# The output gate stored as rows, and the latents split a granule later, in a decoder layer on one core

## The chip, the core and the metric

The kernel runs on one core of one Trainium2 chip. The core has a matrix engine (TensorE, PE in the profile), a vector engine (VectorE, DVE), an activation engine (ScalarE, ACT), GpSimd (POOL), and a sync engine (SyncE, SP) that issues most transfers here. Each engine works through its own queue of instructions in order, and semaphores tie the queues together. Transfers run on 16 DMA engines. TensorE accumulates into PSUM, eight banks of 128 x 512 float32; everything else works in SBUF, 128 partitions wide.

The metric is the device time of one execution in microseconds (us), the median of several.

## The reference

One layer of a decoder with two token mixers in parallel, for one sequence of 512 tokens, D = 2048, in float32.

```python
shift, scale, gate = split(silu(c) @ w_ada + b_ada, 3)        # c: one vector of 2048 for the sequence
h = rmsnorm(x, attn_norm_g) * (1 + scale) + shift
q_lat, kv_lat, k_rope, z_mla, u, v, z_sgu, g_mla, g_sgu = split(h @ w_in)   # widths 768, 512, 64, 6 x 2048

# A: causal attention, 16 heads, from normalised latents
q  = rmsnorm(q_lat, q_norm_g) @ w_uq          # per head 128 + 64 rotary
kv = rmsnorm(kv_lat, kv_norm_g) @ w_ukv       # per head 128 (k) + 128 (v)
y_mla = attention(q, [k | rope(k_rope)], v) * silu(z_mla)
# B: spatial gating in chunks of 128 tokens, 16 groups
y_sgu = u * (tril(w_spatial) @ rmsnorm(v, sgu_norm_g) + b_spatial) * silu(z_sgu)

merged = sigmoid(g_mla) * y_mla + sigmoid(g_sgu) * y_sgu
out = rmsnorm(x + gate * (merged @ w_out), final_norm_g)
```

## The kernel before

**Precision.** Every float32 product is made of three TensorE matmuls on high and low halves (`mm3`: high x high, high x low, low x high). ScalarE makes the high half by a cast, VectorE the low half by a subtraction (`hilo`). Weights come through `Stream`: SP loads 512 KB pieces into three raw buffers in turn (`wraw`, line 98), ScalarE casts each (L117), VectorE subtracts (L118), into one of two pairs, `w0h`/`w0l` and `w1h`/`w1l`. `get(i, ahead)` splits up to piece i + ahead and lets SP load as far as there are free raw buffers. `load_before(piece, f)` hangs another transfer into SP's queue just ahead of that piece's load. SP's queue is in order: an issue that waits for a semaphore holds everything behind it.

**Stages.** In the profiled execution the vectors and the first projection columns come first, then the column blocks (to about 1087 us), the attention heads (to about 1410), the output projection (to the end).

**Column blocks.** The other columns of `h @ w_in` are made in 11 blocks of 28 granules, each granule 24 matmuls, in a scheme that saves products by sums of quarters of the weights. So ScalarE and VectorE split many sums there (ScalarE casts at L620, VectorE subtractions recorded at L135). Everything else that has to happen beside this is in a table of events: `on(s, phase, f)` sets a function at granule s, where s counts up to 0, the first step of attention. In each granule the phases run in the order

```python
FIRST, HIGH, EVAC, GATE, SPLIT, BACK, MISC, LOAD = range(8)
```

with the granule's matmuls between BACK and MISC. The order of the calls is the order in each engine's queue. Ten latent vectors (`latn_d`, 128 x 512 each, six for q and four for k and v) are normalised earlier and kept in DRAM. Near the end of the blocks they come back: `lat_fetch(i)` loads one into a tile `b`, and `lat_split(i)` makes its high half `hh` on ScalarE (scaled by a gain) and its low half `hl` on VectorE. `first_weights` loads the first attention weights, and `split_to(gr[0])` splits the first of them.

**Attention.** Sixteen heads, each with projections of q, k and v from the latents, scores, softmax, transposes, the product with v (`pv`) and the merge with the other mixer. The last head has no next head to prepare; in the places of its projections it runs the first three granules of the output projection.

**Output projection.** The product with `w_out` has four groups of 512 columns, cg = 0 to 3; the first three are done in eight granules each, i = 0 to 7 (`out_granule`, 24 matmuls in four PSUM banks, banks 0 to 3 and 4 to 7 in turn). Granules (0,0), (0,1) and (0,2) lie in the last head, so 21 follow it. Weights `go[cg, i]` come through `Stream` and some of the fourth group's among them. The list `later` holds functions that are called after a granule, by the step 8 * cg + i - 3. The fourth group is done row block by row block at the end, each followed by the final norm and the store of its output rows.

**The gate.** The third part of the adaLN vector is made late. Element j * 128 + p of it is the dot product of row j * 128 + p of the transposed `w_ada` with silu(c). VectorE makes these as multiply-and-sum over a 128-row chunk (one column of `dots` for each of 16 chunks), so the gate comes out as columns: chunk j is column j of `gate`, one element in each partition. The first 8 columns (NG = 8) are made in pieces of 512 during the heads (`piece_sum`); after the last head a reduction over the four pieces and `gate_sum`, which adds the bias, finish them. The other eight follow during the output projection (`chunk_load`, `chunk_sum`) at the steps of `chunk_at` (5, 7, 9, 10 for columns 8 to 11; 11 to 14 for columns 12 to 15).

The residual step needs the gate along the free axis, the same in all partitions. So it goes through DRAM: `gate_store` writes columns a to b to `gate_row`, and `grow_load(cg)` reads 512 of them back as one row broadcast to 128 partitions (`grow`, named `gbc` in the trace). SP issues both. For the first eight columns both stand right behind the last head; then come the gain vector, and, hung between the weight loads of the next granules, `cact` (silu(c), 1 MB), the four row blocks of `xn` (x again, 1 MB each) and the first chunks. For column groups 2 and 3 the store stands one step behind the last `chunk_sum` of the group and the load one step behind that.

Of the kernel before, what the change touches and what calls it, by code (L numbers as in the profile page):

```python
# [11 lines left out]
F32 = mybir.dt.float32  # L12
# [4 lines left out]
ALU = mybir.AluOpType  # L17
AX = mybir.AxisListType
PSUM = bass.MemoryType.PSUM

P = 128
D = 2048
S = 512
KC = D // P
# [18 lines left out]
V7 = [(p, i) for i in range(4) for p in (1, 6)] + [(p, i) for i in range(4) for p in (2, 7)]  # L43
# [8 lines left out]
NG = 8  # L52
# [75 lines left out]
def trunk_layer(ctx, tc, xT, xn, c, vecs, pos, wada, w1, w2, wv, wv3, wv4, wh, wh15, wq, wqr, wk, wvv, wo, wsT, bsp, gfin, out,  # L128
                dbg=None):
    nc = tc.nc  # L130
    ACT, DVE, PE, DMA = nc.scalar, nc.vector, nc.tensor, nc.sync
    LEFT, RIGHT = "left", "right"

    def tt(out, in0, in1, op):
        DVE.tensor_tensor(out=out, in0=in0, in1=in1, op=op)  # L135
# [32 lines left out]
    def nt(p, shape, dt, tag, **kw):  # L168
        uid[0] += 1
        return p.tile(shape, dt, tag=tag, name=f"{tag}_{uid[0]}", **kw)  # L170
# [11 lines left out]
    ws = Stream(nc, [(wp, f"wraw{i}") for i in range(3)], [(wp, f"w{i}") for i in range(2)])  # L182
# [8 lines left out]
    ident = nt(cst, [P, P], F32, "ident")  # L191
# [13 lines left out]
    gate = nt(cst, [P, KC], F32, "gate")  # L205
    dots = nt(cst, [P, 3 * KC], F32, "dots")
# [11 lines left out]
    def scratch(name, shape):  # L218
        return dram.tile(shape, F32, name=name, tag=name)

    gate_row = scratch("gate_row", [KC, P])
# [43 lines left out]
    gq, gr, gk, gvv = {}, {}, {}, {}  # L265
# [45 lines left out]
    def get(i, ahead=1, run=1):  # L311
        r = ws.get(i, ahead)
        fs, pend[:] = pend[:run], pend[run:]
        for f in fs:
            f()
        return r
# [8 lines left out]
    def bank_at(k):  # L325
        return nt(psp.p, [P, S], F32, f"ps{k}")

    def bank():
        n_bank[0] += 1
        return bank_at(ring[(n_bank[0] - 1) % len(ring)])  # L330
# [333 lines left out]
    def gate_sum(a, b):  # L664

        cols = slice(a, b)
        tt(gate[:, cols], dots[:, 2 * KC + a:2 * KC + b], vec[:, C_BADA + 2 * KC + a:C_BADA + 2 * KC + b], ALU.add)

    def gate_store(a, b):
        DMA.dma_start(gate_row[a:b].rearrange("k p -> p k"), gate[:, a:b])  # L670

    def v_norm():
        DVE.tensor_reduce(out=rv, in_=ssv, axis=AX.X, op=ALU.add)
# [15 lines left out]
    FIRST, HIGH, EVAC, GATE, SPLIT, BACK, MISC, LOAD = range(8)  # L689

    def on(s, phase, f, *a):
        assert s >= done[0], (s, done)
        events.setdefault(s, {}).setdefault(phase, []).append(lambda: f(*a))
# [7 lines left out]
    def place(s, us, f, *a):  # L701

        def full(s):
            own, (a, b) = busy.get(s, 0.0) + us, (busy.get(s + d, 0.0) for d in (-1, 1))
            return own > 3.3 or own + max(a, b) > 5.75

        while full(s):
            s += 1
        spend(s, us)
        on(s, BACK, f, *a)  # L710
        return s
# [11 lines left out]
    n_v = len(V7)  # L723
# [28 lines left out]
    rows = {}  # L752
# [199 lines left out]
    for g in range(H):  # L952
# [3 lines left out]
        a = s_ + 4  # L956
        on(a, BACK, sgu_scale)
        a = place(a, 0.29, sgu_weights)
        a = place(a, 0.29, sgu_weights_split)
        if g + 1 < H:  # L960
            on(a + 1, LOAD, sgu_load, g + 1)
        a = place(max(a, s_ + 5), 0.69, sgu_gain)
        a = place(a + 1, 0.69, sgu_split)
# [233 lines left out]
    for group in (((10, "lat8"), (11, "lat9")), ((12, "lat10"), ("plain", "sinT"))):  # L1197
# [9 lines left out]
        i = group[0][0]  # L1207
# [107 lines left out]
    s_att = max(V7.index((2, 3)) + 1 - n_v, s_lat + 1)  # L1315
    on(s_att, LOAD, to_attention)
    for i in range(10):
        on(s_att + i // 2, LOAD, lat_fetch, i)
        on(V7.index((3, 3)) + 1 - n_v + i // 2 if i < 8 else -4, BACK, lat_split, i)

    def first_weights(n):
        ws.limit = gr[0] + n
# [1 line left out]

    for n, s_ in enumerate((-7, -5, -3, -1)):
        on(s_, LOAD, first_weights, n)
    on(-1, SPLIT, lambda: ws.split_to(gr[0]))
    on(-1, MISC, lambda: ws.split_to(gq[0]))
    ws.next_raw, ws.next_part = 0, 1

# [2 lines left out]
    for b in range(len(BLOCKS)):  # L1333
        if b == 1:
            ring[:], n_bank[0] = [5, 6], 0
        for g, (p, i) in enumerate(V7):
# [23 lines left out]
            for k in range(2):  # L1360
                xh, xl = rights[p](2 * i + k)
                st, sp = i == k == 0 and p in (1, 5, 6), i == 3 and k == 1
# [41 lines left out]
    partial = dots[:, 0:4 * NG].rearrange("p (j q) -> p j q", q=4)  # L1404
# [21 lines left out]
    def pieces_at(h):  # L1426
        k = (2 * h, 26, 26, 29)[max(h - 12, 0)]
        for i in range(k, k + (2, 0, 3, 3)[max(h - 12, 0)]):
            piece_sum(i)
# [202 lines left out]
    def out_granule(cg, i, banks, ahead=1, run=1):  # L1632
        wH, wL = get(go[cg, i], ahead, run)
        for k in range(2):
            j = 2 * i + k
            sl = slice(k * 512, (k + 1) * 512)
            for n in range(NB):
                tk = slice(n * P, (n + 1) * P)
                mm3(banks[n], mh[j][:, tk], ml[j][:, tk], wH[:, sl], wL[:, sl], j == 0, j == H - 1)

    for h in range(H):
        if h == H - 1:
            ring[:], n_bank[0] = [4, 5, 6, 7], 0
        dst = scores(h)
        more, odd = h + 1 < H, h % 2 == 1
        pair = h // 2 + 1
        first = go[0, 0] if not more else gr[pair] if not odd and 2 * pair < H else None
        pr_, shares_ = softmax(h, dst, (lambda: ws.split_to(first)) if first is not None else None)
        if more:
            qproj(h + 1, lambda: merge(1 if h == H - 2 else None))  # L1650
            if not odd and 2 * pair < H:
                rps = rproj(pair)
        else:
            pso = [bank_at(k) for k in range(NB)]
            for i in range(2):
                out_granule(0, i, pso)
        pa, fa = transposes(pr_, (0,))
        fa()
        if h < GATED:
            for n in range(NB):  # L1660
                g_ = gt[h][:, n * P:(n + 1) * P]
                ACT.activation(g_, g_, AF.Copy, scale=shares_[:, n:n + 1])
        pb, fb = transposes(pr_, (1,))
        fb()
        pc, fc = transposes(pr_, (2, 3))
        fc()
        if more:
            kps = kproj(h + 1)
            kfinish(h + 1, kps)
        else:  # L1670
            merge()
            pieces_at(h)
            out_granule(0, 2, pso)
        gate_ = gt[h]
        if h < GATED:
            gate_ = nt(tp, [P, S], F32, "sig", bufs=3)
            ACT.copy(gate_, turn(gt[h]))
        tps = turn(vt[h])
        ops = pv(h, {**pa, **pb, **pc})
        merge_a(h, ops, tps, gate_)  # L1680
        if not odd:
            pieces_at(h)
        if not odd and 2 * pair < H:
            m2 = at("m2", F32)
            swapped(m2, rps)
        if more and odd:
            rfinish(pair, rps, m2)
            vproj(pair)
    merge()
    DVE.tensor_reduce(out=dots[:, 2 * KC:2 * KC + NG], in_=partial, axis=AX.X, op=ALU.add)  # L1690
    gate_sum(0, NG)
    gate_store(0, NG)
    gd.close()
    hp.close()
    latp.close()
# [10 lines left out]
    chunks, later = {}, {}  # L1706
# [16 lines left out]
    chunk_at = dict(zip(range(NG, KC), (5, 7, 9, 10, 11, 12, 13, 14)))  # L1723
    for j, st in chunk_at.items():
        later.setdefault(st, []).append(lambda j=j: chunk_sum(j))
        if j + 2 < KC:
            later[st].append(lambda j=j: chunk_load(j + 2))
    for cg in range(NG // 4, 4):
        st = chunk_at[4 * cg + 3]
        later.setdefault(st + 1, []).append(lambda cg=cg: gate_store(4 * cg, 4 * cg + 4))  # L1730
        later.setdefault(st + 2, []).append(lambda cg=cg: grow_load(cg))
    for j in range(NG, NG + 2):
        load_before(go[1, j - NG], chunk_load, j)
# [147 lines left out]
```

## Time and profile before

| | us |
| --- | --- |
| median of 3 runs (1593.01, 1593.63, 1597.45) | 1593.63 |
| the profiled execution | 1595.34 |
| its span in the trace | 1593.60 |
| TensorE busy | 1563.6 (98% of the span) |
| VectorE busy | 1220.5 (77%) |
| ScalarE busy | 801.4 (50%) |
| GpSimd busy | 69.5 (4%) |

The mean clock that TensorE was granted was 0.994 of full speed. The DMA engines moved 316.16 MB, on average 198 GB/s over the span. The profiled execution's time is 1.74 us longer than its span, for what lies around the program. All times of views are in us from the start of the span; line numbers are those of the kernel before. A matmul at a lowered clock counts as busy for longer, so the busy share alone does not say how much of the time is lost.

### The profile page before, as it was taken

How to read it: one execution, taken by the hardware profiler on the slowest of the kernel's cores; microseconds unless marked ns; L12 is line 12 of the kernel's file. 1: busy time of each engine (PE TensorE's matmuls, PEld its weight loads, DVE VectorE, ACT ScalarE, POOL GpSimd, SP SyncE). 2: the span in 40 equal slices, each digit the busy share in tenths (PEclk: the TensorE clock that was granted, in tenths of full speed). 3: DMA queues.
4: the chain of work that ended last, by engine and by line, in shares of the span. 5: the costliest groups of instructions: out<-in, count | busy, mean ns of one | idle time of the engine just before them, and what ended most of it. 6: DMA issues, size and time to landing. Idle time of an engine off the chain costs nothing. (4 is left out here: it accounts for less than half of the span.)

```text
span 1593.6 us, 20601 instructions
## 1 busy us (share of the span) xinstructions
PE 1563.6 (98%) x7397; PEld 1299.8 (82%) x7397; DVE 1220.5 (77%) x1662; ACT 801.4 (50%) x1238; POOL 69.5 (4%) x67
## 2 busy tenths in 40 slices
PE   8999999999999999999999999999999999999998
PEld 7888778888888878888888888877888888878777
DVE  7989777677888889788888788777777778836643
ACT  4445555546544546454545564656566655422222
POOL 0000000201010101020201010100000000000000
PEclk9999999999999999999999999999999999999999
DMA  9979575949695969695948596865333434248722
GB/s 381 360 265 345 164 196 164 245 133 289 214 230 170 237 194 236 193 235 180 229 146 237 183 241 195 215 215 175 120 116 110 126 110 127 89 143 332 207 84 106
DMA packets 239288, 316.16 MB, mean 198 GB/s; under 512 B 18281, under 2 KB 186257, under 8 KB 233553
## 3 DMA queue, kind: packets, MB, share of 16 engines
q1 hardware_dynamic: 216130, 291.25, 55.9%
q0 software_dynamic: 22912, 23.07, 9.5%
q8 instruction: 58, 0.95, 0.3%
q10 hardware_dynamic: 144, 0.52, 0.1%
q14 instruction: 44, 0.36, 0.1%
HBM read 291.11 MB, written 23.68 MB: 198 GB/s over the span
## 5 line engine op out<-in xcount | busy, mean ns | idle before, releaser
L135 DVE TENSOR_TENSOR X<-X,X 128x1024 fp32r<-128x1024 f32 (+2 forms) x110 | 129.4, 1181 | 29.5 <-ACT X L620 26.6
L620 ACT CAST w0h<-X 128x1024 fp32r<-128x1024 f32 x70 | 73.6, 1051 | 95.0 <-PE ps L1366 61.4
L620 ACT CAST X<-X 128x1024 fp32r<-128x1024 f32 x69 | 72.5, 1051 | 89.7 <-PE ps L1366 54.0
L620 ACT CAST w1h<-X 128x1024 fp32r<-128x1024 f32 x70 | 73.6, 1052 | 82.5 <-PE ps L1366 44.2
L135 DVE TENSOR_TENSOR w0l<-X,w0h 128x1024 fp32r<-128x1024 f32 x70 | 85.5, 1221 | 27.1 <-ACT w0h L620 26.8
L135 DVE TENSOR_TENSOR w1l<-X,w1h 128x1024 fp32r<-128x1024 f32 x70 | 85.5, 1222 | 26.1 <-ACT w1h L620 25.6
L118 DVE TENSOR_TENSOR w0l<-wraw,w0h 128x1024 fp32r<-128x1024 f32 (+4 forms) x61 | 64.2, 1053 | 53.3 <-ACT w0h L117 51.6
L147 PE MATMUL ps<-hh,w1h 128*128 128x512 f32 (+1 forms) x260 | 103.4, 398 | 1.7 <-ACT hh L425 1.4
L148 PE MATMUL ps<-hl,w1h 128*128 128x512 f32 (+1 forms) x260 | 101.6, 391 | 0.5 <-DVE hl L138 0.5
L149 PE MATMUL ps<-hh,w1l 128*128 128x512 f32 (+1 forms) x260 | 101.5, 391 | 0.0
L117 ACT CAST w0h<-wraw 128x1024 fp32r<-128x1024 f32 (+4 forms) x61 | 55.9, 917 | 83.6 <-issue 21.9
L135 DVE TENSOR_TENSOR X<-wraw,X 128x1024 f32<-128x1024 f32 (+1 forms) x66 | 80.6, 1221 | 19.6 <-ACT X L620 17.0
L1367 PE MATMUL ps<-w1l,hh 128*128 128x512 f32 x236 | 92.3, 391 | 2.5 <-DVE w1l L135 2.5
L1367 PE MATMUL ps<-w0l,hh 128*128 128x512 f32 x236 | 92.3, 391 | 1.8 <-DVE w0l L135 1.7
L147 PE MATMUL ps<-hh,w0h 128*128 128x512 f32 x238 | 93.7, 394 | 0.0
L148 PE MATMUL ps<-hl,w0h 128*128 128x512 f32 x238 | 92.8, 390 | 0.0
L149 PE MATMUL ps<-hh,w0l 128*128 128x512 f32 x238 | 92.7, 390 | 0.0
L1365 PE MATMUL ps<-w0h,hh 128*128 128x512 f32 x236 | 92.1, 390 | 0.1
L1365 PE MATMUL ps<-w1h,hh 128*128 128x512 f32 x236 | 91.9, 390 | 0.2 <-ACT w0h L620 0.2
L138 DVE SCALAR_TENSOR_TENSOR wada<-wada,cact 128x2048 f32<-128x2048 f32 x39 | 88.9, 2282 | 4.1 <-DMA wada<-in_wada 4.1
L1366 PE MATMUL ps<-w0h,hl 128*128 128x512 f32 x236 | 91.9, 389 | 0.0
L1366 PE MATMUL ps<-w1h,hl 128*128 128x512 f32 x236 | 91.9, 389 | 0.0
(395 smaller groups left out, 4348.9 us busy)
## 6 DMA issues: line engine op xcount, KB each, us to landing
X<-in_wh SPq DMA_DIRECT2D x131, 512.0 KB, 4.7
wada<-in_wada SPq DMA_DIRECT2D x39, 1024.0 KB, 7.7
wraw<-in_wo SPq DMA_DIRECT2D x32, 512.0 KB, 5.0
wraw<-in_wh SPq DMA_DIRECT2D x21, 512.0 KB, 5.6
wraw<-in_wh POOLq DMA_DIRECT2D x21, 512.0 KB, 8.1
X<-in_wv SPq DMA_DIRECT2D x17, 512.0 KB, 3.7
X<-in_wh SPq DMA_DIRECT2D x22, 384.0 KB, 3.6
half<-in_w SPq DMA_DIRECT2D x32, 256.0 KB, 5.2
```

The lines of the kernel that those rows point to most:

```text
L117: self.nc.scalar.copy(hi[:, :n], raw[:, :n])
L118: self.nc.vector.tensor_tensor(out=lo[:, :n], in0=raw[:, :n], in1=hi[:, :n].bitcast(F32), op=ALU.subtract)
L135: DVE.tensor_tensor(out=out, in0=in0, in1=in1, op=op)
L138: DVE.scalar_tensor_tensor(out=out, in0=in0, scalar=scalar, in1=in1, op0=op0, op1=op1, **kw)
L147: PE.matmul(ps, ah, bh, start=start, stop=False)
L148: PE.matmul(ps, ah, bl, start=False, stop=False)
L149: PE.matmul(ps, al, bh, start=False, stop=stop)
L620: ACT.copy(hi, t)
L1365: PE.matmul(ps[t].rearrange("p (h w) -> p h w", h=4), xh[:, tk], wH[:, k], start=st, stop=False, skip_group_check=True)
L1366: PE.matmul(ps[t].rearrange("p (h w) -> p h w", h=4), xl[:, tk], wH[:, k], start=False, stop=False, skip_group_check=True)
L1367: PE.matmul(ps[t].rearrange("p (h w) -> p h w", h=4), xh[:, tk], wL[:, k], start=False, stop=sp, skip_group_check=True)
```

## The change

**The gate.** `gate_store` is gone. In its place `gate_turn` lets TensorE transpose the finished columns (128 x 8 or 128 x 4) into a PSUM bank, and VectorE copies the result (8 x 128 or 4 x 128) to a tile `sig`; SP then writes rows of 128 consecutive elements to `gate_row`. For the first eight columns the reduction and `gate_sum` stand ahead of granule (0,2) in the last head, and the turn and store right behind that granule. For groups 2 and 3 the turn stands where the store stood, in a bank named by number (1 and 4), the store a step later, and `grow_load` a step after that, one step later than before.

**The latents.** `lat_fetch` is called for three latents in a granule instead of two. `lat_split` of two latents a granule moves from granules -8 to -4 to granules -7 to -3. In granule -1, `split_to(gr[0])` goes from phase SPLIT to phase HIGH.

```diff
--- before.py
+++ after.py
@@ -666,8 +666,11 @@
         cols = slice(a, b)
         tt(gate[:, cols], dots[:, 2 * KC + a:2 * KC + b], vec[:, C_BADA + 2 * KC + a:C_BADA + 2 * KC + b], ALU.add)
 
-    def gate_store(a, b):
-        DMA.dma_start(gate_row[a:b].rearrange("k p -> p k"), gate[:, a:b])
+    def gate_turn(a, b, pg, row):
+
+        PE.transpose(pg[:b - a, :P], gate[:, a:b], ident)
+        DVE.tensor_copy(row[:b - a, :P], pg[:b - a, :P])
+        return lambda: DMA.dma_start(gate_row[a:b], row[:b - a, :P])
 
     def v_norm():
         DVE.tensor_reduce(out=rv, in_=ssv, axis=AX.X, op=ALU.add)
@@ -1315,8 +1318,8 @@
     s_att = max(V7.index((2, 3)) + 1 - n_v, s_lat + 1)
     on(s_att, LOAD, to_attention)
     for i in range(10):
-        on(s_att + i // 2, LOAD, lat_fetch, i)
-        on(V7.index((3, 3)) + 1 - n_v + i // 2 if i < 8 else -4, BACK, lat_split, i)
+        on(s_att + i // 3, LOAD, lat_fetch, i)
+        on(i // 2 - 7, BACK, lat_split, i)
 
     def first_weights(n):
         ws.limit = gr[0] + n
@@ -1324,7 +1327,7 @@
 
     for n, s_ in enumerate((-7, -5, -3, -1)):
         on(s_, LOAD, first_weights, n)
-    on(-1, SPLIT, lambda: ws.split_to(gr[0]))
+    on(-1, HIGH, lambda: ws.split_to(gr[0]))
     on(-1, MISC, lambda: ws.split_to(gq[0]))
     ws.next_raw, ws.next_part = 0, 1
 
@@ -1670,7 +1673,10 @@
         else:
             merge()
             pieces_at(h)
+            DVE.tensor_reduce(out=dots[:, 2 * KC:2 * KC + NG], in_=partial, axis=AX.X, op=ALU.add)
+            gate_sum(0, NG)
             out_granule(0, 2, pso)
+            gate_turn(0, NG, bank(), nt(tp, [P, S], F32, "sig", bufs=3))()
         gate_ = gt[h]
         if h < GATED:
             gate_ = nt(tp, [P, S], F32, "sig", bufs=3)
@@ -1687,9 +1693,6 @@
             rfinish(pair, rps, m2)
             vproj(pair)
     merge()
-    DVE.tensor_reduce(out=dots[:, 2 * KC:2 * KC + NG], in_=partial, axis=AX.X, op=ALU.add)
-    gate_sum(0, NG)
-    gate_store(0, NG)
     gd.close()
     hp.close()
     latp.close()
@@ -1725,9 +1728,12 @@
         later.setdefault(st, []).append(lambda j=j: chunk_sum(j))
         if j + 2 < KC:
             later[st].append(lambda j=j: chunk_load(j + 2))
-    for cg in range(NG // 4, 4):
-        st = chunk_at[4 * cg + 3]
-        later.setdefault(st + 1, []).append(lambda cg=cg: gate_store(4 * cg, 4 * cg + 4))
+    rows = []
+    for cg, k in ((2, 1), (3, 4)):
+        st = chunk_at[4 * cg + 3] + 1
+        later.setdefault(st, []).append(lambda cg=cg, k=k: rows.append(
+            gate_turn(4 * cg, 4 * cg + 4, bank_at(k), nt(tp, [P, S], F32, "sig", bufs=3))))
+        later.setdefault(st + 1, []).append(lambda: rows.pop()())
         later.setdefault(st + 2, []).append(lambda cg=cg: grow_load(cg))
     for j in range(NG, NG + 2):
         load_before(go[1, j - NG], chunk_load, j)
```

The next rows show the queues of three engines as written, before and now. A row names the line, the operation, the tiles written and read, and the size.

VectorE in the last head, before. `piece` and `dots` are the gate's last partial sums, `w0l` and `w1l` low halves of split weights, the first `sig` the merge of the head, `dots` at L1690 the reduction and `gate` the finished columns:

```order
L138 SCALAR_TENSOR_TENSOR piece_12118,dots_93<-piece_12118,cq_11389 128x512
L118 TENSOR_TENSOR w0l_12266<-wraw_99_12076,w0h_12265 128x1024
L135 TENSOR_TENSOR sig_12313<-ps_1851_12300,g_1787_11810 128x512
L135 TENSOR_TENSOR sig_12313<-sig_12313,ps_1850_12295 128x512
L135 TENSOR_TENSOR g_1854_12317<-sig_12313,b_1853_12316 128x512
L1690 TENSOR_REDUCE dots_93<-dots_93 128x8
L135 TENSOR_TENSOR gate_92<-dots_93,vec_88 128x8
```

And the same place now (the `sig` of 8x128 is the gate as rows, the others the merge):

```order
L138 SCALAR_TENSOR_TENSOR piece_12118,dots_93<-piece_12118,cq_11389 128x512
L1676 TENSOR_REDUCE dots_93<-dots_93 128x8
L135 TENSOR_TENSOR gate_92<-dots_93,vec_88 128x8
L118 TENSOR_TENSOR w0l_12268<-wraw_99_12076,w0h_12267 128x1024
L672 COPY sig_12298<-ps_1850_12297 8x128
L135 TENSOR_TENSOR sig_12320<-ps_1853_12307,g_1787_11810 128x512
```

The reduction and the sum moved from behind the merge to ahead of the split of a weight, and the copy of the turned gate is new between that split and the merge.

SP at the store of column group 2, before (`wraw`: weight loads, `wada`: a chunk for later gate columns, `gbc`: the row read back):

```order
L670 DMA gate_row<-gate_92 128x4x1
L98 DMA wraw_115_12765<-in_wo 128x1024
L1714 DMA wada_12792<-in_wada 128x2048
L1710 DMA gbc_12329<-gate_row 128x512
L98 DMA wraw_116_12807<-in_wo 128x1024
```

And SP at the same place now:

```order
L673 DMA gate_row<-sig_12765 4x128
L98 DMA wraw_116_12814<-in_wo 128x1024
L98 DMA wraw_117_12816<-in_wo 128x1024
L1713 DMA gbc_12333<-gate_row 128x512
L98 DMA wraw_118_12852<-in_wo 128x1024
```

The store now stands behind the weight load and the chunk load that it was ahead of, and two further weight loads stand between it and the load that reads it.

ScalarE at the first latents, near the end of the column blocks, before (`X` and `w1h`: high halves of column weights, `hh`: high halves of latents, `d`: an activation of a result):

```order
L620 CAST X_1328_8668<-X_1310_8578 128x1024
L1295 ACTIVATE hh_1330_8675<-b_1317_8618,vec_88 128x512
L1295 ACTIVATE hh_1332_8679<-b_1318_8620,vec_88 128x512
L620 CAST w1h_8701<-wraw_1236_8104 128x1024
L844 ACTIVATE d_1285_8401<-d_1285_8401 128x1024
```

And ScalarE at the same place now:

```order
L620 CAST X_1331_8674<-X_1310_8578 128x1024
L620 CAST w1h_8697<-wraw_1236_8104 128x1024
L847 ACTIVATE d_1285_8401<-d_1285_8401 128x1024
L1298 ACTIVATE hh_1338_8702<-b_1317_8618,vec_88 128x512
L1298 ACTIVATE hh_1340_8706<-b_1318_8620,vec_88 128x512
```

The first pair of latent halves moved behind one cast of a column weight and one activation.

## The prediction

> **What bounds the kernel now.** I read the page's engine line first, then busy time by stretches, then TensorE's waits, then the chain of waits behind them.
>
> ```profile
> PE 1563.6 (98%) x7397; PEld 1299.8 (82%) x7397; DVE 1220.5 (77%) x1662; ACT 801.4 (50%) x1238; POOL 69.5 (4%) x67
> ```
>
> TensorE is the bound, and every matmul is needed. This change adds three small ones and removes none, so it can only win what TensorE loses: idle time and a lowered clock. The next table shows where. Its columns are start:end and length, busy time and count of PE, PEld, DVE, ACT and POOL, granted clock, DMA share, GB/s.
>
> ```profile
> 1100.00:1380.00 280.00, 279.21 (x1669) 247.56 (x1668) 216.40 (x460) 161.68 (x373) 0.00 (x0) 1.00 0.39 123
> 1458.40:1485.60 27.20, 27.20 (x121) 22.52 (x120) 20.83 (x22) 7.44 (x10) 0.00 (x0) 1.00 0.82 274
> 1418.86:1535.26 116.40, 105.85 (x433) 84.90 (x432) 62.75 (x66) 30.02 (x40) 0.00 (x0) 0.94 0.76 248
> 1061.18:1087.00 25.82, 22.98 (x97) 17.71 (x96) 22.77 (x28) 18.32 (x25) 0.00 (x0) 1.00 0.56 189
> ```
>
> The attention heads lose nothing. The second row is the output projection undisturbed: five granules of 24 matmuls in 27.20 us, 5.44 us each or 0.2267 us a matmul. The third row is 18 granules of it, 432 matmuls (the 433rd hangs over the edge): 18 x 5.44 = 97.92, so 116.40 - 97.92 = **18.5 us are lost**. The fourth row is the end of the column blocks, just ahead of attention: 96 x 0.2267 = 21.76, so **4.1 us are lost**. TensorE's waits, first in 1380 to 1594, then in 1000 to 1110:
>
> ```profile
> PE ps L147 <- ACT w0h L117: 5.6, 2, 3.2
> PE ps L147 <- ACT w1h L117: 2.5, 1, 2.5
> PE ps L1367 <- DVE w0l L135: 1.4, 1, 1.4
> PE ps L1367 <- DVE w1l L135: 1.3, 1, 1.3
> ```
>
> In the projection it waits for weights to be split, and the splits wait for loads. The chain there, in order of time (start, length), and SP's own wait:
>
> ```profile
> 1411.28 10.51 DMA gate_row<-gate
> 1427.68 16.74 DMA wraw<-in_wo
> ...
> 1479.85 11.54 DMA gate_row<-gate
> 1491.88 6.09 DMA wraw<-in_wo
> ...
> 1509.37 10.11 DMA wraw<-in_wo
> SPq L1710 <- DMA gate_row<-gate: 21.6, 3, 10.1
> ```
>
> Each column store of the gate takes 10.5 to 11.5 us to land, SP waits 21.6 us for them at `grow_load`, and all weight loads stand behind it in SP's queue. The store also holds up what is issued after it: the load of 1509.37 took 10.1 us with SP free. In the three stretches behind the stores the DMA engines moved almost nothing:
>
> ```profile
> 1412.50:1421.50 9.00, 9.00 (x41) 7.45 (x40) 2.45 (x2) 2.11 (x2) 0.00 (x0) 1.00 0.05 2
> 1485.50:1491.50 6.00, 6.00 (x29) 4.95 (x27) 3.76 (x3) 1.05 (x1) 0.00 (x0) 1.00 0.96 75
> 1510.00:1517.50 7.50, 7.50 (x35) 6.21 (x34) 3.69 (x5) 1.78 (x3) 0.00 (x0) 1.00 0.51 32
> ```
>
> The first only waits; in the other two loads were queued (share 0.96 and 0.51) and moved 75 and 32 GB/s.
>
> **Part 1: the gate as rows.** The three stalls, two granules each (10.88 us if undisturbed), a fourth small one, and the clock behind the three:
>
> ```profile
> 1424.30:1441.35 17.05, 13.09 (x49) 10.07 (x48) 2.45 (x2) 2.09 (x2) 0.00 (x0) 0.90 1.01 399
> 1491.04:1507.19 16.15, 12.87 (x49) 9.98 (x48) 9.16 (x12) 4.95 (x7) 0.00 (x0) 0.89 0.74 237
> 1512.63:1529.82 17.19, 14.29 (x49) 10.90 (x48) 9.15 (x11) 5.42 (x8) 0.00 (x0) 0.80 0.63 177
> 1452.24:1458.40 6.16, 5.76 (x25) 4.43 (x24) 5.06 (x7) 1.66 (x3) 0.00 (x0) 1.00 0.83 301
> 1435.30:1438.65 3.35, 3.35 (x10) 2.57 (x9) 0.00 (x0) 0.38 (x1) 0.00 (x0) 0.50 1.03 429
> 1500.15:1503.50 3.35, 3.07 (x7) 2.48 (x8) 3.32 (x5) 1.23 (x2) 0.00 (x0) 0.50 0.52 157
> 1520.65:1527.40 6.75, 6.25 (x14) 4.59 (x15) 5.67 (x7) 2.61 (x4) 0.00 (x0) 0.50 0.51 168
> ```
>
> They cost 6.2, 5.3, 6.3 and 0.7 us, together the 18.5. Of these, 13.45 us at half clock are 6.7 us. [...] The waits here were 3.2, 2.5 and 2.4 us and the clock fell after all three, so I follow the trace: no gap, no half clock.
>
> The new store has a twin in this kernel, the turn of the SGU gains to rows:
>
> ```profile
> 265.38:271.32 5.94, 5.94 (x27) 4.65 (x26) 3.57 (x4) 2.42 (x4) 0.00 (x0) 1.00 0.43 132
> L766 SPq DMA_DIRECT2D gain_row<-sig x1: 329/329/329, 268.9 to 268.9; - x1
> DMA to landing us min/median/max: 1.4/1.4/1.4
> L765 ACT COPY vec<-ps x1: 158/158/158, 268.7 to 268.7; 128x16 f32<-128x16 f32 x1
> ```
>
> A 16-row store landed in 1.4 us. Two transposes lengthened 24 matmuls (5.44) to 5.94, 0.25 us each; three cost **0.7 us** (0.3 if they hide in the group of four that follows the first, 1.5 if each waits for VectorE). The copies out of PSUM are bounded by that 0.16 us copy and by a 128x512 multiply, 0.69 us. VectorE at the last head, before (start, length, idle ahead):
>
> ```profile
> 1404.85 1.22 DVE L118 TENSOR_TENSOR w0l<-wraw,w0h 128x1024 fp32r<-128x1024 f32 x1
> 1408.11 0.69 DVE L135 TENSOR_TENSOR sig<-ps,g 128x512 f32<-128x512 f32 x1 [2.04 <-PE ps L149]
> 1410.87 0.18 DVE L1690 TENSOR_REDUCE dots<-dots 128x8 f32<-128x32 f32 x1
> 1411.08 0.17 DVE L135 TENSOR_TENSOR gate<-dots,vec 128x8 f32<-128x8 f32 x1
> ```
>
> Its 2.0 us idle ahead of the merge hold the copy (first pair of order rows, with the change). Sum and gate moved up from behind the merge, ahead of `w0l`, and the copy stands where the idle time was. The copy waits for TensorE to end granule 2; the merge behind it waits longer anyway, for the `pv` matmuls. `w0l` is 0.35 us later and TensorE needs it after `pv`, so that is covered too. On SP (second pair of order rows, at the second store) the store moved behind a weight load and a chunk load, and two more weight loads, each held by a split, stand between it and its reader, a granule apart: 5.4 us against 1.4. The third store gains the same distance. Its copy stands ahead of two splits on VectorE and waits for the end of granule (2,2); those splits are due a granule later, so the delay is covered. If one of the two came late, its granule would stall as the second does now. The first store now leaves near 1407 (1404.85 + 0.35 + 1.22, the copy and the issue) and lands near 1409 instead of 1421.8, so `grow_load`, the vectors, `xn` and the weights go out some 12 us earlier. I take all **18.5 us** (bounds: 12.3 if the first stall stays, 18.5).
>
> **Part 2: the latents split a granule later.** What stalled there, ScalarE in order of time:
>
> ```profile
> 1065.95 1.38 ACT L1295 ACTIVATE hh<-b,vec 128x512 fp32r<-128x512 f32 x2 [2.01 <-DMA b<-latn_d]
> 1067.23 1.04 ACT L620 CAST w1h<-wraw 128x1024 fp32r<-128x1024 f32 x1
> 1069.98 1.39 ACT L1295 ACTIVATE hh<-b,vec 128x512 fp32r<-128x512 f32 x2 [0.75 <-DMA b<-latn_d]
> 1071.27 1.03 ACT L620 CAST w0h<-X 128x1024 fp32r<-128x1024 f32 x1
> 1078.28 1.04 ACT L620 CAST w1h<-X 128x1024 fp32r<-128x1024 f32 x1
> ```
>
> The first `hh` sits in the queue 2.0 us before its latent lands, and the casts of the column weights wait behind it. In the third pair of order rows (`X`, `w1h`: column weights; `hh`: latent halves; `d`: an activation of a result) a latent pair no longer stands ahead of a `w1h` cast. The first pair moved behind a cast and an activation, and every later pair likewise, with its VectorE half. SP's third fetch passes one column-weight load, which goes out an issue (0.4 us) later and is cast only at 1078. Following both queues with these lengths (1.0 a cast, 0.66 a split half), `w0h` ends near 1068.6 instead of 1072.3 and its stall goes (4.1 split as the waits, 1.4 to 1.3, is 2.1 and 2.0). `w1h` ends near 1076.8 instead of 1079.3, but TensorE arrives 2.1 us sooner, so I leave about 1 us there and 0.3 at the last granule: 4.1 - 1.3 = **2.8 us** gained (bounds: 4.1 if all is covered, 1.5 lost if the last pair, now at -3, delays the first attention weights). Moving the first attention split ahead on VectorE covers that.
>
> **Sum.** 18.5 - 0.7 + 2.8 = 20.6 us. The profiled execution took 1595.34 (span 1593.60 and 1.74 around it); 1595.3 - 20.6 = **1574.7 us**. The median of the runs, 1593.63, is 1.7 below that execution, about what half of one 3.35 us half-clock stretch costs. I sum against the profiled execution, since the lost time is measured in it.
>
> **Rivals.**
> - *The first stall returns as a burst* (0.10). The rows (0.75 MB), `cact` (1 MB), two chunks and `xn` (1 MB each piece) still go out between the weights. For: the DMA engines were full at 399 GB/s there. Against: it starts 12 us sooner. At 399 GB/s the load issued near 1412, behind 1.75 MB, lands near 1416 for a split near 1424, and the next two loads fare alike: 7 us to spare. 1574.7 + 6.2 = 1580.9.
> [...]
> - *The shift of the latents backfires* (0.05): 1574.7 + 2.8 + 1.5 = 1579.0.
> - *The row stores still choke the DMA* (0.05): only SP's wait goes, the last two stalls stay: 1574.7 + 11.6 = 1586.3.
> - *Slower* (0.05): the burst meets the loads for granules (0,7), (1,0), (1,1) and (1,2), and each stalls as the first does now, 4 x 6.2 = 24.8: 1599.5. It decides once a load, issued near 1412 for a split near 1424, takes over 12 us. The worst now took 8.3:
>
> ```profile
> 1423.69 0.38 SPq L98 DMA_DIRECT2D wraw<-in_wo  x1
> 1432.03 1.04 ACT L117 CAST w0h<-wraw 128x1024 fp32r<-128x1024 f32 x1 [11.90 <-DMA wraw<-in_wo]
> ```
>
> **How the numbers follow.** The forecast has 0.70. The range goes from 1571 (all of part 2, transposes hidden, and the 2.3 us by which the fastest run lies below the profiled one) to 1583, over the first three rivals. A measurement of this kernel can tell 0.3%, 4.8 us, from no change: faster means below 1588.9. The forecast and the first three rivals are faster, the fourth by about half its chance (0.02; with the first stall kept as well it gives 1592.5), so 0.92; same 0.03; slower 0.05.
>
> **What would show it.** Right: `gate_row` lands in under 3 us, SP waits nothing at `grow_load`, granules of 5.44 us from 1419 on, clock 1.00 until the tail, one PE wait of about 1 us near 1078. Wrong: PE waits for `w0h` or `w1h` in the projection, a half-clock stretch without a gap, or a wait at the first attention projections.

## The result, and the profile after

Over its runs the changed kernel takes 1576.89 us (median of four, 1574.67 to 1578.5), beside 1595.54 for the kernel before in the same comparison: a ratio of **0.9883** (95% interval 0.9861 to 0.9905). The profiled execution took 1576.21 us, its span 1574.5.

The changed kernel's page, engine line first: TensorE's share rises from 98% to 99%, with three more matmuls.

```profile
PE 1558.1 (99%) x7400; PEld 1297.6 (82%) x7400; DVE 1221.5 (78%) x1665; ACT 801.4 (51%) x1238; POOL 70.3 (4%) x67
```

Busy time by stretches, columns as in the prediction's table (the eighth field, ahead of DMA share and GB/s, is the granted clock). The stretches begin and end with the same matmuls as before: the entry to attention, the 18 granules, the two granules that stalled first, and the start of the program.

```profile
1062.93:1085.80 22.87, 22.39 (x98) 17.87 (x97) 21.35 (x26) 18.26 (x25) 0.00 (x0) 1.00 0.62 207
1417.82:1516.04 98.22, 98.22 (x435) 81.10 (x434) 62.97 (x68) 30.43 (x40) 0.00 (x0) 1.00 0.74 270
1423.26:1440.30 17.04, 17.04 (x77) 14.12 (x76) 6.50 (x7) 4.37 (x6) 0.00 (x0) 1.00 1.00 405
20.00:23.40 3.40, 3.40 (x9) 2.63 (x8) 3.36 (x5) 1.45 (x3) 0.00 (x0) 0.50 1.03 419
```

The 18 granules take 98.22 us instead of 116.40, TensorE is busy in all of it and the clock is 1.00. The third row is the place of the first stall: the DMA engines are as full as before (405 GB/s), but nothing waits; the burst of transfers started earlier. The entry takes 22.87 instead of 25.82. The last row lies far ahead of all that was edited: a half-clock stretch in the first projection, where the kernel before had clock 1.00 in its profile. It cost 1.7 us in this execution. The same stretch before:

```profile
20.00:23.40 3.40, 3.40 (x16) 2.80 (x16) 3.36 (x5) 1.63 (x3) 0.00 (x0) 1.00 1.02 416
```

TensorE's waits, in the projection and at the entry:

```profile
PE ps L148 <- DVE w0l L118: 0.8, 1, 0.8
PE ps L1370 <- DVE w1l L135: 0.5, 1, 0.5
```

The first belongs to granule (0,1), which the change does not touch; of the entry's two waits (1.4 and 1.3) 0.5 is left. The two casts of column weights that were late at the entry:

```profile
1069.21 1.03 ACT L620 CAST w0h<-X 128x1024 fp32r<-128x1024 f32 x1
1077.08 1.04 ACT L620 CAST w1h<-X 128x1024 fp32r<-128x1024 f32 x1
```

SP in order of time at the first store, and its wait for the rows:

```profile
1405.75 0.32 SPq L673 DMA_DIRECT2D gate_row<-sig  x1
1409.15 0.81 SPq L1713 DMA_DIRECT2D gbc<-gate_row  x2
SPq L1713 <- DMA gate_row<-sig: 5.4, 2, 3.0
```

The store left at 1405.75 and its row could be read at 1409.15; before, it left at 1411.28 and the reader went out at 1421.85. SP still waits at `grow_load`, but 5.4 us in all instead of 21.6.

From stage to stage, the two profiled executions compare so (starts of the same matmuls):

| up to | before | after | difference | change in it |
| --- | --- | --- | --- | --- |
| last granules of the blocks | 1061.19 | 1062.93 | +1.74 | +1.74 (clock at 20 us) |
| first attention projection | 1087.01 | 1085.80 | -1.21 | -2.95 (latents) |
| granule (0,5) | 1418.87 | 1417.82 | -1.05 | +0.16 (first turn 0.11) |
| granule (2,7) | 1535.26 | 1516.04 | -19.22 | -18.17 (gate rows) |
| end of the span | 1593.60 | 1574.47 | -19.13 | +0.09 |

### The profile page after: what moved, and what is told of

The parts are those of the page before. It is cut to its first block, busy times and chain, and to the rows that moved or that the text cites. A ratio compares the mean times of both kernels' runs of the same rounds, so it can differ in the third digit from the quotient of the medians.

```text
span 1574.5 us, 20617 instructions
## 1 busy us (share of the span) xinstructions
PE 1558.1 (99%) x7400; PEld 1297.6 (82%) x7400; DVE 1221.5 (78%) x1665; ACT 801.4 (51%) x1238; POOL 70.3 (4%) x67
## 5 line engine op out<-in xcount | busy, mean ns | idle before, releaser
L117 ACT CAST w1h<-wraw 128x1024 fp32r<-128x1024 f32 (+4 forms) x60 | 50.5, 841 | 83.2 <-issue 23.9
```

The source lines that it names most:

```text
L117: self.nc.scalar.copy(hi[:, :n], raw[:, :n])
```

## The experiments

**The two parts, each alone.** `rows_only` is the changed kernel with this undone:

```diff
-        on(s_att + i // 3, LOAD, lat_fetch, i)
-        on(i // 2 - 7, BACK, lat_split, i)
+        on(s_att + i // 2, LOAD, lat_fetch, i)
+        on(V7.index((3, 3)) + 1 - n_v + i // 2 if i < 8 else -4, BACK, lat_split, i)
...
-    on(-1, HIGH, lambda: ws.split_to(gr[0]))
+    on(-1, SPLIT, lambda: ws.split_to(gr[0]))
```

> The changed kernel with the latents' part undone (fetch, split and first attention split as before); the gate goes as rows. Theory (the two parts are independent, the gate's stores are the projection's whole loss): the projection's 18 granules take 98.2 us, all at full clock, and the entry to attention keeps 25.8 us with PE waits of 1.4 us for w0l and 1.3 for w1l. That is 18.2 less than before: a ratio of 0.9886. Rival (the latents' part shifts the projection's start against the loads and so takes part in its gain): a stall of over 2 us returns in the projection and the ratio is above 0.990.

`latents_only` is the kernel before with these lines as in the change.

> The kernel before with the latents' part alone. Theory: the entry to attention takes 22.9 us instead of 25.8, the three stalls of the projection stay with 6.2, 5.3 and 6.3 us, total 2.9 us less, a ratio of 0.9982. Rival (its gain is given back at the first stall of the projection, since TensorE arrives there earlier and waits for the same landing): the entry is shorter, the total unchanged, a ratio of 1.000.

Measured: `rows_only` 1577.6 us, ratio 0.9871 (0.9858 to 0.9884); `latents_only` 1596.02 us, 0.9985 (0.9977 to 0.9994). The entry, and the projection from granule (0,5) on, of each:

```profile
1061.24:1086.34 25.10, 22.70 (x98) 17.78 (x96) 22.81 (x28) 18.35 (x25) 0.00 (x0) 1.00 0.55 190
1418.24:1516.47 98.23, 98.23 (x436) 81.10 (x434) 62.98 (x68) 30.22 (x40) 0.00 (x0) 1.00 0.76 270
```

```profile
1061.15:1083.42 22.27, 22.22 (x97) 17.86 (x96) 21.36 (x26) 18.25 (x25) 0.00 (x0) 1.00 0.62 210
1415.32:1529.41 114.09, 101.08 (x409) 81.18 (x408) 61.19 (x65) 28.97 (x39) 0.00 (x0) 0.93 0.77 250
```

With the rows alone the projection loses nothing and the entry is nearly as before, so the rival of `rows_only` falls. With the latents alone the entry is short, but the projection loses more than before: the second stretch, 17 granules here (408 matmuls), takes 114.09 where 92.48 would do, so 21.6 are lost instead of 18.5. The first two stalls are longer, 8.6 and 6.4 us instead of 6.2 and 5.3. So of the 3.55 us won at the entry, 3.1 were given back in this execution (the spans are 1593.2 and 1593.6), much as the rival of `latents_only` said. Over its eleven runs the ratio still stands for 2.4 us won (1.0 to 3.7). The latents' gain is safe only where the stalls are gone: in the changed kernel it is kept up to the end, as the table of stages shows. The totals do not show it there: the ratio of `rows_only`, 0.9871, is not above the 0.9883 of the whole change, and the two intervals overlap.

**Which of the store's two harms.** The prediction named two: SP waits for the landing, and loads queued behind the store crawl. `columns_moved` keeps the change's places and times, but stores element by element:

```diff
-        PE.transpose(pg[:b - a, :P], gate[:, a:b], ident)
-        DVE.tensor_copy(row[:b - a, :P], pg[:b - a, :P])
-        return lambda: DMA.dma_start(gate_row[a:b], row[:b - a, :P])
+        return lambda: DMA.dma_start(gate_row[a:b].rearrange("k p -> p k"), gate[:, a:b])
```

> The changed kernel in its new places, but with the element-by-element column store and without the three transposes and copies. Theory W (SP's wait at the load of the row starves the splits; the new distance is what cures it): stores still land after 10 to 11 us, SP waits some 5 us less at each load of the row, the stalls go but for 0 to 2 us each: 1577 to 1580 us, a ratio of 0.990. Theory C (the column store itself holds up the weight loads that are queued behind it on the DMA engines): the first stall goes or shrinks, since that store leaves some 5 us earlier, and the second and third stay with 5 to 6 us each, with loads of about 10 us behind the stores: 1588 us, a ratio of 0.9955.

`no_wait` leaves the kernel before as it is and takes SP's wait at `grow_load` away, by reading other data, so that the residual is scaled by a wrong row:

```diff
-... bass.AP(tensor=gate_row.tensor, offset=gate_row.offset + cg * S, ap=[[0, P], [1, S]]))
+... bass.AP(tensor=gfin.tensor, offset=gfin.offset + cg * S, ap=[[0, P], [1, S]]))
```

> The kernel before with the column stores where they were, but the loads of the row read the final norm's gain instead of the stored gate (the residual is scaled by the wrong row), so that SP waits for no store. Theory W: all four stalls of the projection go, a ratio of 0.9885. Theory C: loads behind the stores still take 8 to 10 us, the second and third stalls stay with 4 to 6 us each and the first with 1 to 6, a ratio of 0.993 to 0.998.

Measured: `columns_moved` 1587.9 us, ratio 0.994 (0.9927 to 0.9954); `no_wait` 1594.6 us, 0.9978 (0.9969 to 0.9987). The first, by stretches (the first stall's place with the granules after it, the second, the third, all 18 granules), and SP's wait at `grow_load`:

```profile
1422.58:1452.49 29.91, 28.40 (x122) 22.22 (x120) 13.31 (x15) 6.49 (x9) 0.00 (x0) 1.00 1.01 400
1485.13:1503.11 17.98, 14.26 (x49) 10.89 (x48) 8.46 (x11) 4.80 (x6) 0.00 (x0) 0.81 0.77 168
1513.99:1526.86 12.87, 11.47 (x49) 8.94 (x48) 5.66 (x6) 2.85 (x5) 0.00 (x0) 1.00 0.54 177
1417.14:1526.86 109.72, 103.08 (x433) 82.60 (x432) 62.73 (x66) 30.03 (x40) 0.00 (x0) 0.97 0.79 264
SPq L1711 <- DMA gate_row<-gate: 21.7, 3, 10.6
```

Less 5.44 a granule, the places lose 2.7, 7.1 and 2.0 us, together 11.8. New places without new form win a third. SP waited as long as before (21.7 us, before 21.6), so this run shows what the form costs and cannot tell the wait from the slow loads; `no_wait` has to. Theory C had the total (1588), but not the parts: it expected 5 to 6 us each at the second and third place, and no run separates why one lost more and the other less. In `no_wait`, the 18 granules, two loads behind the second and third store in the chain of waits (start, length), and a wait of SP:

```profile
1419.71:1536.39 116.68, 106.97 (x434) 85.56 (x432) 62.86 (x66) 30.12 (x40) 0.00 (x0) 0.93 0.75 244
1484.86 12.73 DMA wraw<-in_wo
1508.99 11.42 DMA wraw<-in_wo
SPq L98 <- DMA gate_row<-gate: 8.2, 1, 8.2
```

In this execution, the slowest of the ten, 116.68 - 97.92 = 18.8 us are still lost; by the ratio the missing waits win 3.5 us. At the first store a weight load still waited 8.2 us for the landing, so the first stall (4.05 us) cannot tell the wait from the slow loads. At the second and third, SP waited for no store, and TensorE lost 6.9 and 7.0 us there, more than the 5.3 and 6.3 before: loads issued behind a store took 11 to 13 us. Theory W falls, theory C stands: what had to go was the store's form. Freed of the wait, SP only queues the loads sooner behind the same obstruction.

**What is slow in the form.** `probe` is the changed kernel with one store added in each of eleven heads, and with waits of TensorE, of which the last section tells:

```diff
+        DMA.dma_start(d.rearrange("k p -> p k"), vec[:, 0:n])          # side by side: d is [n, P]
+        DMA.dma_start(d[:, :, 0].rearrange("k p -> p k"), vec[:, 0:n])  # 512 B apart: d is [n, P, P]
...
+        nc.gpsimd.dma_start(dot0[0:1, 0:1], src)                        # src: one element of d
...
+        PE.transpose(a[:, :P], ident, ident)
+        DVE.tensor_copy(b[:, :P], a[:, :P])
+        for _ in range(n):
+            tt(b[:, :P], b[:, :P], ident, ALU.mult)
+        PE.transpose(a[:, :P], b[:, :P], ident)
```

> The changed kernel with two additions that leave its output alone. In heads 3 to 13, SP also stores something to scratch rows, one store a head, and GpSimd reads one element back (its wait shows the landing): element by element 128, 256, 512, 1024 and 2048 elements into adjoining places; 8 rows of 512 B; 512 and 1024 elements 512 B apart; 128 pieces of 16, 64 and 256 B. Theory N (the time goes by the number of elements): landing grows in proportion, 512 elements about half of 1024, and the distance apart changes nothing. Theory B (adjoining small writes are slow behind the DMA engines, since 512 and 1024 elements landed in 10.6 to 11.5 and 10.5 us alike): 512 and 1024 elements land in 8 to 12 us alike, and 512 B apart in under 5 us. In the output projection, TensorE is made to wait six times, for chains of 1 to 11 small VectorE instructions, about 0.5 to 3 us. Theory (a wait of about 2.4 us is enough): the half clock follows the waits of 2.4 us and more and none under 1.5 us. [...]

GpSimd's read of a store shows when it had landed. SP's issues first (128 and 2048 elements side by side, 1024 elements 512 B apart), then GpSimd's reads of the same three, in order of time:

```profile
1131.10 0.42 SPq L1458 DMA_DIRECT2D pr<-vec  x1
1206.86 0.43 SPq L1458 DMA_DIRECT2D pr<-vec  x1
1256.99 0.43 SPq L1461 DMA_DIRECT2D pr<-vec  x1
...
1139.71 0.56 POOL L1469 DMA_DIRECT2D dot<-pr  x1 [115.85 <-DMA pr<-vec]
1221.49 0.50 POOL L1469 DMA_DIRECT2D dot<-pr  x1 [26.91 <-DMA pr<-vec]
1262.62 0.51 POOL L1469 DMA_DIRECT2D dot<-pr  x1 [10.85 <-DMA pr<-vec]
```

Side by side, 128 elements took 8.6 us and 2048 took 14.6: sixteen times the number, not twice the time. 1024 elements 512 B apart took 5.6. Theory N falls. Theory B has the direction right and the sizes in part: 512 and 1024 elements side by side took 11.1 and 12.8 us, 512 elements 512 B apart 6.5, not under 5. The 128 pieces of 16, 64 and 256 B took 5.2, 3.6 and 6.3; of the 8 rows the record shows nothing, since GpSimd waited for its own read before it. `no_wait_apart` puts that into the kernel before, with as many elements and the same places:

```diff
-        DMA.dma_start(gate_row[a:b].rearrange("k p -> p k"), gate[:, a:b])
+        DMA.dma_start(gate_wide[a:b, :, 0].rearrange("k p -> p k"), gate[:, a:b])   # [KC, P, P]
```

> The kernel before with the same element-by-element stores at the same places and in the same number, but each element 512 B from the next in DRAM, and the loads of the row reading the final norm's gain instead (as in the run that took SP's wait away; the residual is scaled by the wrong row). Theory B (elements side by side in one row are what is slow): the stores land in 5 to 7 us, loads behind them take 5 to 6 us, the second and third stalls go, and the ratio is 0.988 to 0.991. Rival (any store of 512 elements holds up the loads behind it): the stalls of 6 to 7 us stay, a ratio of about 0.998 as in the run without SP's wait.

Measured: 1577.18 us, ratio 0.9895 (0.9875 to 0.9915). Its 18 granules, and the landing of its stores; the second landing row is that of `no_wait`:

```profile
1418.25:1516.17 97.92, 97.92 (x433) 81.08 (x432) 62.51 (x66) 30.22 (x40) 0.00 (x0) 1.00 0.78 283
DMA to landing us min/median/max: 2.5/4.4/7.4
```

```profile
DMA to landing us min/median/max: 11.9/12.1/13.2
```

Nothing is lost at all. The only difference from `no_wait` is where the elements go, 512 B apart in a wider scratch array, so the obstruction (loads of 12.73 and 11.42 us) came here from stores of 512 4-byte elements side by side. Why the memory behaves so, no run shows.

**Is the extra granule needed?** In `rows_tight` the second and third row stores follow their turn at once, and the reader comes a step later, as before the change:

```diff
-        later.setdefault(st + 1, []).append(lambda: rows.pop()())
-        later.setdefault(st + 2, []).append(lambda cg=cg: grow_load(cg))
+        later.setdefault(st, []).append(lambda: rows.pop()())
+        later.setdefault(st + 1, []).append(lambda cg=cg: grow_load(cg))
```

> The changed kernel with the second and third row store right behind their turn and the load of the row one granule behind, as before the change. Theory (landing in some 3 us is what matters, the extra granule is only room): SP waits at each store for the granule's end and the copy, the weight loads behind it go out up to 5 us later, but raw buffers are ahead by more: stalls of 0 to 1 us, a ratio to before within 0.001 of the changed kernel's 0.988. Rival (the extra granule is needed): two stalls of 2 to 5 us, a ratio of 0.991 to 0.994.

Measured: 1575.22 us, ratio 0.9865 (0.9849 to 0.9881), a little below what was expected. SP's waits and the 18 granules:

```profile
SPq L673 <- DVE sig L672: 3.5, 2, 2.6
SPq L1713 <- DMA gate_row<-sig: 3.0, 1, 3.0
1416.64:1514.87 98.23, 98.23 (x436) 81.10 (x434) 63.05 (x68) 30.32 (x40) 0.00 (x0) 1.00 0.75 269
```

SP waits for the copies, up to 2.6 us each, and no granule notices: the granule of distance is worth nothing once the store is a row.

**The latents, once more.** `split_only` fetches two a granule as before and splits a granule later:

```diff
-        on(s_att + i // 3, LOAD, lat_fetch, i)
+        on(s_att + i // 2, LOAD, lat_fetch, i)
```

> The changed kernel with the latents fetched two a granule as before, and split a granule later as now. Theory (the order of the splits is what cured the entry): entry 22.9 us as in the changed kernel. Rival (the earlier fetch is needed, since ScalarE still waits for a latent to land): ScalarE waits 1 to 2 us for a latent ahead of a cast, and the entry is 0.5 to 2 us longer.

`latents_two_later` splits one more granule later:

```diff
-        on(i // 2 - 7, BACK, lat_split, i)
+        on(i // 2 - 6, BACK, lat_split, i)
```

> The changed kernel with the latents split one granule later still (granules -6 to -2). Theory (latent pairs that stand ahead of the column weights' halves are what is left of the loss): the wait of 0.5 us for w1l at the entry goes or shrinks, entry 22.0 to 22.5 us from the w1 granule at 1063 to the first attention projection instead of 22.9. Rival (the last pairs now meet the first attention weights): the wait moves to the first attention projections, which start 0 to 1.5 us later than in the changed kernel.

`after_again` is the changed kernel, in another comparison.

> The changed kernel once more, to stand beside the others of this row of runs: a ratio of 0.987 to 0.989, the projection's 18 granules in 98.2 us, entry 22.9 us.

`split_only` took 1575.64 us and `latents_two_later` 1574.19, one run each. The entry of `split_only`; the entry of `after_again` and ScalarE's wait in it; the entry of `latents_two_later` and its first two attention projections:

```profile
1060.90:1085.30 24.40, 22.65 (x98) 17.79 (x96) 21.54 (x26) 18.53 (x25) 0.00 (x0) 1.00 0.61 203
```

```profile
1061.87:1086.35 24.48, 22.62 (x97) 17.79 (x96) 21.53 (x26) 18.43 (x25) 0.00 (x0) 1.00 0.61 204
1072.16 0.72 ACT L1298 ACTIVATE hh<-b,vec 128x512 fp32r<-128x512 f32 x1 [2.06 <-DMA b<-latn_d]
```

```profile
1061.33:1083.11 21.78, 21.78 (x98) 17.98 (x96) 20.10 (x24) 18.39 (x25) 0.00 (x0) 1.00 0.65 221
1083.11:1095.37 12.26, 11.17 (x50) 8.93 (x48) 9.01 (x12) 10.04 (x14) 0.00 (x0) 1.00 0.65 192
```

`after_again` (1575.72 us, ratio 0.9883, 0.9868 to 0.9899) missed its expectation at the entry: 24.48 instead of 22.9, because one latent landed later and ScalarE waited 2.06 us for it. So the entry of one kernel varies by 1.6 us between executions, and `split_only`'s 24.40 cannot say what the earlier fetch is worth; that stays open. Nor does a run show what the earlier split of the first attention weight (phase HIGH) is worth by itself. Six profiles have the change's latents: 22.87 and 24.48 in the changed kernel, 22.27, 22.56, 22.79 and 23.95 in `latents_only`, `columns_moved`, `rows_tight` and `probe`, mean 23.2. Four have the old ones: 25.82 before, 25.10, 25.06 and 25.33 in `rows_only`, `no_wait` and `no_wait_apart`, mean 25.3. The two groups do not overlap. `latents_two_later` empties the entry, and gives back 0.45 of it (12.26 instead of 11.81) at the first attention projections, as its rival said.

**What was left.** `best` puts the last pair behind the first attention weights, and splits the weight of granule (0,1) earlier:

```diff
-        on(i // 2 - 7, BACK, lat_split, i)
+        on((-6, -5, -4, -3, -1)[i // 2], BACK, lat_split, i)
...
-        pr_, shares_ = softmax(h, dst, (lambda: ws.split_to(first)) if first is not None else None)
+        pr_, shares_ = softmax(h, dst, (lambda: ws.split_to(go[0, 1] if h == H - 1 else first)) if first is not None else None)
```

> The changed kernel with two edits for what is left: the latents' pairs split at granules -6, -5, -4, -3 and -1 (the last behind the first attention weights), and the second output projection weight split in the last head's softmax, ahead of two of its exponentials. Theory: the entry takes 21.8 us instead of 22.9, the first attention projections wait for nothing, and granule (0,1) takes 5.5 us instead of 6.7: 2 to 2.5 us less than the changed kernel, a ratio to before 0.0015 below its. Rival (the exponentials are then late for the transposes of the last head, or the last latents for the key projection): one of the two is given back, 1 us or less gained.

Entry, first attention projections, granules (0,0) and (0,1):

```profile
1061.27:1083.05 21.78, 21.78 (x98) 17.98 (x96) 20.09 (x24) 18.38 (x25) 0.00 (x0) 1.00 0.63 219
1083.05:1094.88 11.83, 11.51 (x49) 8.78 (x48) 9.19 (x12) 10.05 (x14) 0.00 (x0) 1.00 0.61 189
1382.82:1394.02 11.20, 11.20 (x50) 8.94 (x50) 7.37 (x20) 4.14 (x10) 0.00 (x0) 1.00 0.44 137
```

1572.28 us (1572.15 to 1572.44), ratio 0.9863 (0.9846 to 0.988). Every run of it lies below every run of `after_again` beside it (1574.0 to 1576.68). The two granules took 12.30 there, so 1.1 us come from the early split and up to 2.7 from the entry; nothing was given back.

## Why the prediction was right, and where it was off

- **The sum.** 1574.7 was forecast for the profiled execution, which took 1576.2. The difference is the 1.7 us of half clock at 20 us, which no step covered, less 0.3 for the turns.
- **Part 1** went as worked out: 18.5 less the turns. Three turns were put at 0.7 and cost 0.11 + 0.13 + 0.13 = 0.37; the two later ones lengthened a granule from 5.44 to 5.57.
- **The landing** was off. The row store was to land in under 3 us and SP to wait for nothing, after a twin that landed in 1.4. SP waited 3.0 and 2.4. The reader of the second store went out 5.8 us after it (1477.34 to 1483.10), so a granule of 5.44 us did not even cover the landing. Why it took longer than its twin no run separates. It cost nothing.
- **The distance of a granule** carried weight in the argument for the second and third stall, and `rows_tight` shows that it had none.
- **Two harms, one cause.** The prediction did not weigh SP's wait against the slow loads behind the store. `columns_moved` came out at 1587.9 where the rival of the choking row stores had its price of 1586.3. That is near by luck: the rival kept two stalls (5.3 and 6.3) and took SP's wait away, while the run lost at three places (2.7, 7.1 and 2.0) and kept the wait. What a choking store costs `no_wait` shows better (6.9 and 7.0); the rival fell because the row stores did not choke (98.22 us for the 18 granules, TensorE busy in all of it).
- **The burst** came with 405 GB/s at the forecast place and stalled nothing. But the room was misjudged. The prediction called 8.3 us the worst load, while its own chain has one of 16.74 (issued at 1427.68), above the 12 us from which its slower rival would begin. In the changed kernel the first load of the burst left at 1411.40 and took 8.1 us, for a split at 1423.45: 4 us to spare, not 7. In `columns_moved`, where the row was read some 7 us later (1416.29) and the burst came behind it, this place lost 2.7 us: the margin was real and not large.
- **Part 2**: 2.8 forecast, 2.95 in the first profile, 1.3 in the second (25.82 to 24.48), 2.4 by the ratio of `latents_only`. The mechanism held: less the 1.74 us of the clock, the two casts ended at 1068.5 and 1076.4, where 1068.6 and 1076.8 were worked out. The size depends on when a latent lands.
- **The half clock** went with the gaps, as forecast: the 18 granules ran at clock 1.00, before at 0.94. With that the chance of 0.05 fell that it would stay without them (1574.7 + 6.7 = 1581.4, the second of the rivals in the order in which the prediction counts them). But the prediction's "no gap, no half clock" says too little of which gaps count: in the probe kernel 2.01 us of idle time in one stretch of 3.41 us were followed by half clock, and 1.53 and 1.29 us in two were not, as the last section shows.

## What to carry to other kernels

A transfer that wrote neighbouring elements one by one harmed this kernel twice, and the worse harm was not its own landing (SP waited 21.6 us at `grow_load`; without that `no_wait` won 3.5 us) but what was queued behind it (in `no_wait` 18.8 us still lost, loads of 11 to 13 us): look at the GB/s of the stretch after it (75 and 32 here, with loads queued), not at the wait that names it. To tell a wait from an obstruction, take the wait away and leave the transfer; if the loss stays, its place is not the main matter (here new places won a third), and its form has to change. Before a gain of a microsecond is credited to an edit, profile the same kernel twice (the entry took 22.87 and 24.48 us in two profiles of this one).

## What the runs showed of the hardware

The clock. The probe kernel also made TensorE wait six times in the projection, and the half clock did not follow the length of the wait. The waits (TensorE's rows, idle ahead of each), and windows of 3.41 us, laid out from where its half-clock stretches begin:

```profile
1473.13 0.33 PE L1766 MATMUL ps<-ident,sig 128*128 128x128 f32 x1 [2.01 <-DVE sig L135]
1488.91 0.33 PE L1766 MATMUL ps<-ident,sig 128*128 128x128 f32 x1 [2.67 <-DVE sig L135]
1520.50 0.33 PE L1766 MATMUL ps<-ident,sig 128*128 128x128 f32 x1 [3.36 <-DVE sig L135]
...
1470.71:1474.12 3.41, 1.40 (x8) 0.91 (x7) 2.79 (x7) 1.04 (x1) 0.00 (x0) 1.00 0.88 308
1474.12:1477.53 3.41, 3.41 (x10) 2.66 (x9) 2.30 (x3) 0.00 (x0) 0.00 (x0) 0.50 0.60 183
1484.36:1487.77 3.41, 1.88 (x9) 1.26 (x7) 2.08 (x7) 1.60 (x2) 0.00 (x0) 1.00 0.81 258
1487.77:1491.18 3.41, 2.12 (x9) 1.66 (x10) 3.31 (x7) 0.39 (x1) 0.00 (x0) 1.00 0.49 186
1515.08:1518.49 3.41, 2.06 (x10) 1.42 (x8) 2.17 (x6) 2.61 (x4) 0.00 (x0) 1.00 0.80 307
1518.49:1521.90 3.41, 1.40 (x7) 1.19 (x8) 3.21 (x8) 0.00 (x0) 0.00 (x0) 1.00 0.04 15
1521.91:1525.32 3.41, 3.41 (x10) 2.64 (x9) 2.53 (x4) 0.72 (x2) 0.00 (x0) 0.50 0.66 208
```

The wait of 2.01 us lay in one window (idle 3.41 - 1.40 = 2.01) and the next window ran at half clock. The wait of 2.67 was split over two (idle 1.53 and 1.29) and the clock stayed at 1.00. The wait of 3.36 idled 1.35 and 2.01 of two windows, and half clock followed the second. Of the other three, those of 0.71 and 1.37 us cost no clock, and one of 6.11 did. The half-clock stretches of six traces (before, after, `latents_only`, `columns_moved`, `no_wait` and `probe`), but for the one that runs into a program's end, last 3.41 us or twice that, and those of one trace begin on one grid: before at 1435.26, 1500.12 and 1520.60 us (1520.60 - 1500.12 = 20.48, six times 3.41), in the probe kernel's projection at 1474.12, 1521.91 and 1535.56 (13.65 from the second to the third, four times 3.41). In the probe kernel, in the projection, windows with 2.01 us idle and more were followed by half clock and those with 1.53 and less were not. In between, one window with 1.94 us idle in the kernel before was not followed, while one with 1.85 in `no_wait` was, and so was one with 1.76 at the start of the probe kernel. These records put the limit no closer than that; a wait of 2.01 us was enough. The expectation that a wait's length decides fell: the 2.67 us wait was above its limit of 2.4 and cost no clock.

The half clock at 20 us in the changed kernel's profile is the same thing at the start: the window ahead of it (16.57 to 19.98) held 1.93 us of idle time. How much falls into one window there changes from execution to execution, with nothing edited up to that place: 2.13 us in `columns_moved` (15.91 to 19.32), with half clock behind it, 1.43 before (15.32 to 18.73) and 1.29 in `latents_only` (14.60 to 18.02), without.
